# Values of four retention heads and of the spatial gating as one block product with seven products

## The chip, the cores and the metric

The kernel runs on one core of one Trainium2 chip. The metric is the device time of a run in microseconds (us). TensorE (PE in the profile) multiplies matrices, VectorE (DVE), ScalarE (ACT) and GpSimd (POOL) work on rows of 128 partitions, and SyncE (SP) issues transfers. "Layer 0" and "layer 1" are the two layers of the network.

## The reference

Two layers over 512 tokens of 1024 features. What matters here is the input projection of a layer: `proj = rms_norm(h) @ w_in`, cut into nine pieces.

```python
sizes = (D_LRU, D_LRU, D_RET, D_RET, D_RET, D_RET, D_SGU, D_SGU, D_SGU)   # 768, 768, 4 x 768, 3 x 512
x_lru, g_lru, q, k, v, g_ret, u_sgu, v_sgu, g_sgu = jnp.split(proj, split_points, axis=-1)
lru_out = rg_lru(causal_depthwise_conv(x_lru, ...), ...)       # 8 blocks of 96 features
ret_out = retention(q, k, v, positions, ret_norm[i])           # 6 heads of 128, chunks of 128 tokens
sgu_out = spatial_gating(u_sgu, v_sgu, ...)                    # LayerNorm of v_sgu, token mixing in chunks
mixed = concatenate([lru_out * silu(g_lru), ret_out * silu(g_ret), sgu_out * silu(g_sgu)])
h = h + mixed @ w_out[i]
z = rms_norm(h, ple_norm[i])
h = h + sigmoid(z @ w_ple_gate[i]) * (p[i] @ w_ple_proj[i])
```

The values `v` of heads 0 to 3 (512 features) and `v_sgu` (512 features) are two products of the same normed activations (512 tokens by 1024) with two blocks of `w_in` (1024 by 512 each).

## The kernel before, in words

All large products are made in split precision. An operand x becomes a high part (a cast to fp32r) and a low part (x minus the high part), and `mm3` (L172 to L174) adds three products: high by high, high by low, low by high. So every tile of weights costs an ACT cast (L131, `whi`) and a DVE subtraction (L132, `wlo`) before PE may use it. Weights arrive as 82 chunks per layer, most of them 128 x 1024 floats, in the fixed order of `plan()`; `take` hands out the next one, and `prefetch` converts chunks up to four ahead of the one in use. The tags `whi` and `wlo` have four buffers, `raw` (as loaded) has two.

The work of PE is cut into steps (`step`): convert weights ahead, the matmuls, some items of a queue `bg` of background work (`n_bg`, three as a rule), then the eviction of the PSUM accumulator by DVE or ACT. Four accumulators (tag `mm`) go round. The program that builds the kernel orders the instructions of each engine itself, by the source order and by what it takes to be ready, so an instruction can stand far ahead of its place in the source; the order is fixed once built. Each engine runs its own list strictly in order.

A layer goes: six `feat_steps` for `x_lru` with a convolution as eviction (`conv`, L449 to L454, results sent by transfers to the tile `U`, then split into `xc`, L459 and L460); `tok_steps` for `v_sgu` (tokens on the partitions, moving operand 256 weights wide, output `vs`); LayerNorm (`ln_apply`); for each of four column tiles c the steps u(c) and gs(c), with the groups of the recurrence (`lru_group`) of three, three and two blocks ahead of c = 0, 1 and 3; `tok_steps` for the values of heads 0 and 1; `sgu_out` (the gated result `sm` times `w_out`, L622 to L631); six retention heads with k, q and gr steps, and `tok_steps` for values ahead of heads 2 and 4; the output gate; the output projection; the embedding gate. Each `tok_steps` takes two chunks and issues 96 matmuls: 2 halves x 2 token tiles x 8 k tiles x 3.

`norm_stat` and `norm_bcast` give 1/rms as the tile `R` (L288), which every eviction of x_lru needs first. `rope_tables` makes the rotary tables once, as background work that enters the queue after the third x_lru step of layer 0.

Of the kernel before, what the change touches and what calls it, by code (L numbers as in the profile page):

```python
# [26 lines left out]
LRU_AT = {0: 0, 1: 1, 3: 2}  # L27
LRU_GROUPS = [(0, 1, 2), (3, 4, 5), (6, 7)]
# [9 lines left out]
def plan():  # L38
    out = []
    for l in range(DEPTH):  # L40
        out += [(l, "in", OFF["xl"] + P * f, 1024) for f in range(6)]
        for c in range(2):
            out += [(l, "inv", (OFF["vs"] + 256 * c, kh), 1024) for kh in range(2)]
        for c in range(4):
            if c in LRU_AT:
                out += [(l, "lg", LRU_AT[c], 2 * LB * len(LRU_GROUPS[LRU_AT[c]]))]
            out += [(l, "in", OFF["u"] + P * c, 1024), (l, "in", OFF["gs"] + P * c, 1024)]
        for h in range(NH):
            if h % 2 == 0:
                out += [(l, "inv", (OFF["v"] + P * h, kh), 1024) for kh in range(2)]  # L50
            if h == 0:
                out += [(l, "osg", f, 1024) for f in range(4)]
            out += [(l, "in", OFF[n] + P * h, 1024) for n in ("k", "q", "gr")]
# [10 lines left out]

def rows(chunk):
    return LB if chunk[1] == "lg" else P


# the slots of the 40 split operand tiles, by layer
SLOTS = [  # L70
    {"y": range(0, 16), "xc": list(range(16, 28)) + list(range(36, 40)), "lru": range(16, 28), "sgu": range(28, 36), "ret": range(28, 40), "p": range(32, 36)},
    {"y": range(16, 32), "xc": range(0, 16), "lru": range(0, 12), "sgu": range(32, 40), "ret": list(range(32, 40)) + list(range(12, 16)), "p": range(0, 4)},
# [5 lines left out]
def trunk(ctx, tc, a):  # L78
# [7 lines left out]
    def f32(t):  # L86
        return t.bitcast(F32)

    def act_tiles(slots, name):
# [5 lines left out]
    chunks = plan()  # L95
    offs = np.concatenate([[0], np.cumsum([rows(c) * c[3] for c in chunks])])
    st = {"raw": 0, "cv": 0, "use": 0}
    raws, ready = {}, {}
# [4 lines left out]
    def emit_raw():  # L103
        i = st["raw"]
        n, m = chunks[i][3], rows(chunks[i])
        r = wp.tile([P, 1024], F32, tag="raw", name=f"raw{i}", bufs=2)
# [3 lines left out]
        raws[i] = r  # L110
        st["raw"] += 1

    def emit_cv():
        i = st["cv"]
        l, kind, _, n = chunks[i]
        r = raws.pop(i)
# [54 lines left out]
    def mm3(out, wh, wl, xh, xl, first, last):  # L171
        T.matmul(out, wh, xh, start=first, stop=False)  # L172
        T.matmul(out, wh, xl, start=False, stop=False)  # L173
        T.matmul(out, wl, xh, start=False, stop=last)  # L174
# [16 lines left out]
    spt = tp.tile([P, S], F32, tag="r0", name="spt", bufs=3)  # L191
# [8 lines left out]
    posi = tp.tile([P, S], I32, tag="m2", name="posi")  # L200
# [17 lines left out]
    def rsqrt(v, n):  # L218
        """1/sqrt(v) of a small [P, n] tile; a bit seed and three Newton steps."""
# [20 lines left out]
    def norm_square(d, c):  # L240
# [3 lines left out]
        if d == 0:  # L244
            nrm["acc"] = tp.tile([P, S], F32, tag="nacc", name="nacc", bufs=1)
# [9 lines left out]
    def norm_stat(t0=0, nt=4, diag=True):  # L255
# [21 lines left out]
        nrm["dg"] = [tp.tile([P, S], F32R, tag=t, name="n" + t, bufs=b) for t, b in (("dg", 1), ("sq", 2))]  # L277
# [17 lines left out]
    def feat_steps(l, y, kinds, evicts, look=LOOK, n_bg=3, mid=None):  # L295
        """The feature tiles of `kinds` together, one pass over the k tiles."""
# [14 lines left out]
    def tok_steps(l, y, off, evict):  # L311
        """256 features with the tokens on the partitions; evict(half, acc[P, 2, 256])."""
# [22 lines left out]
    def silu_scaled(acc, name):  # L335
        """x * sigmoid(x) of x = acc / rms, in an SBUF tile."""
# [8 lines left out]
    cosT = cp.tile([P, S], F32, name="cosT")  # L345
    sinT = cp.tile([P, S], F32, name="sinT")
# [13 lines left out]
    def rope_tables():  # L360
        ang = tp.tile([P, S], F32, tag="m2", name="ang")
        n1 = tp.tile([P, S], F32, tag="r0", name="n1", bufs=3)
        n2 = tp.tile([P, S], F32, tag="r1", name="n2", bufs=3)
# [56 lines left out]
    # ================= the layers =================  # L420
# [10 lines left out]
    for l in range(DEPTH):  # L431
# [1 line left out]
        U = cp.tile([LB, NB, S], F32, tag="U", name="U")  # L433
        xc = act_tiles(SLOTS[l]["xc"], f"xc{l}_")

        def blocks(c):
            """(block, first row in it, first row of tile c, rows) of the pieces of tile c."""
# [7 lines left out]
        def conv(c):  # L445
            def f(acc):
                u = tp.tile([P, S], F32, tag="r1", name=f"xcv{c}", bufs=3)
# [7 lines left out]
                for b in range(NB):  # L455
                    if P * c < LB * b + LB <= P * c + P:

                        def sp(b=b):
                            SC.copy(xc[b][0][:LB], U[:, b, :])  # L459
                            V.tensor_sub(xc[b][1][:LB], U[:, b, :], f32(xc[b][0])[:LB])  # L460

                        bg.append(sp)

            return f

        feat_steps(l, y, [("in", 0), ("in", P)], [conv(0), conv(1)], mid=norm_finish)
        for c in range(2, 6):
            feat_steps(l, y, [("in", P * c)], [conv(c)])
            if l == 0 and c == 2:
                softplus()  # L470
                bg.extend(rope_tables())
        rn = nrm["rn"]

# [9 lines left out]
        vs = [tp.tile([P, 4, 256], F32, tag="v4", name=f"vs{c}") for c in range(2)]  # L483
# [15 lines left out]
        def ln_apply():
# [7 lines left out]
            for c in range(2):  # L507
                for t in range(4):
                    V.tensor_scalar(vs[c][:, t, :], vs[c][:, t, :], mv[:, t, 0:1], r[:, t : t + 1], op0=ALU.subtract, op1=ALU.mult)
# [9 lines left out]
        def lru_group(g):  # L519
# [3 lines left out]
            def gate_step(gate, b):  # L523
# [10 lines left out]
                def ev():  # L534
                    t = tp.tile([P, S], F32, tag=f"r{gate}", name=f"rg{gate}{b}", bufs=3)[:LB]
# [12 lines left out]
            def tanh_exp():  # L548
                for b in grp:
                    Ts[b] = tp.tile([P, S], F32, tag="r1", name=f"lT{b}", bufs=3)[:LB]  # L550
# [4 lines left out]
            def sqrts():  # L555
                for o, b in enumerate(grp):
                    sTs[b] = tp.tile([P, S], F32, tag="sq" if o < 2 else "dg", name=f"sT{b}", bufs=2 if o < 2 else 1)[:LB]
# [15 lines left out]
        for c in range(2):  # L573
            tok_steps(l, y, OFF["vs"] + 256 * c, vs_evict(c))
# [335 lines left out]
```

## Time and profile before

| what | value |
|---|---|
| three runs | 928.05, 928.16 (median), 928.65 us |
| span of the profiled execution, first to last instruction | 926.7 us |
| PE busy | 912.6 us, 98% of the span |
| DVE busy | 644.3 us, 70% |
| ACT busy | 406.7 us, 44% |
| matmuls | 4786 |

The profile gives the span as the time of the profiled execution; the runs are timed from outside and are some 1.5 us longer than the span. "Busy" for PE counts the time in which some matmul is under way; matmuls overlap, so a group's mean duration is longer than the distance from one start to the next.

### The profile page before, as it was taken

Reading aid. Unit: us, or ns where it says so; the run is one execution under the profiler, and the core shown is the slowest. Engines: PE = TensorE matmul, PEld = TensorE weight load, DVE = VectorE, ACT = ScalarE, POOL = GpSimd, SP = SyncE. Lnnn points to the kernel's source line nnn. Section 1 sums busy time; section 2 is a strip of 40 time slices with the busy share of each in tenths; the row PEclk is TensorE's granted clock in tenths of the full one; section 3 lists DMA queues with packets and bytes.
Section 4 is the critical chain, followed back from the end, with each engine's and each line's share of the span. In section 5 each row is a group of like instructions: output and inputs, shape, how many; then the busy total and the mean of one; then the engine's idle time right before and its main releaser. Section 6 shows DMA issues by size and latency. Waiting matters only on the chain.

```text
span 926.7 us, 12415 instructions
## 1 busy us (share of the span) xinstructions
PE 912.6 (98%) x4786; PEld 778.4 (84%) x4786; DVE 644.3 (70%) x1252; ACT 406.7 (44%) x595; POOL 37.8 (4%) x33
## 2 busy tenths in 40 slices
PE   7999999999999999999999999999999999999997
PEld 5797888888898888888889888988989888888886
DVE  7999996566667774446669699746586777534564
ACT  5349984223233343444434687412323234433353
POOL 3000000000000000110200000000000000011020
PEclk9999999999999999999999999999999999999999
DMA  6452234322222342342334313333222333233312
GB/s 211 128 154 69 61 104 137 93 90 69 92 86 85 109 119 87 108 137 78 104 105 129 104 52 114 98 94 103 71 76 64 111 89 116 86 103 97 125 46 92
DMA packets 31355, 92.60 MB, mean 100 GB/s; under 512 B 4224, under 2 KB 4672, under 8 KB 31296
## 3 DMA queue, kind: packets, MB, share of 16 engines
q1 hardware_dynamic: 27312, 85.42, 29.1%
q10 hardware_dynamic: 3984, 6.38, 2.5%
q8 instruction: 37, 0.61, 0.3%
q14 instruction: 22, 0.18, 0.1%
HBM read 83.40 MB, written 2.10 MB: 92 GB/s over the span
## 4 chain that ended last, share of the span: by engine, by line
PE 88%; DVE 5%; ACT 3%; DMA 1%; issue 1%; DVEq 0%; ACTq 0%
PE acc L174 27%; PE acc L172 27%; PE acc L173 27%; PE sc L680 1%; PE o L705 1%; DVE wlo L132 1%; DMA raw<-in_wall 1%; PE o L707 1%; PE kv L692 1%; PE pp L174 1%; DVE y L237 1%; PE pp L173 1%; PE pp L172 1%; DVE U L567 1%; PE oT L728 1%
## 5 line engine op out<-in xcount | busy, mean ns | idle before, releaser
L131 ACT CAST whi<-raw 128x1024 fp32r<-128x1024 f32 (+1 forms) x160 | 157.9, 990 | 356.7 <-PE acc L173 241.0
L132 DVE TENSOR_TENSOR wlo<-raw,whi 128x1024 fp32r<-128x1024 f32 (+3 forms) x164 | 187.2, 1142 | 104.4 <-ACT whi L131 104.2
L172 PE MATMUL acc<-y,whi 128*128 128x512 f32 x608 | 241.5, 397 | 0.7 <-DVE whi L129 0.6
L173 PE MATMUL acc<-y,whi 128*128 128x512 f32 x608 | 237.7, 391 | 3.0 <-DVE y L237 2.9
L174 PE MATMUL acc<-y,wlo 128*128 128x512 f32 x608 | 237.8, 391 | 0.4 <-DVE wlo L132 0.2
L173 PEld LDWEIGHTS acc<-y,whi 128*128 128x128 f32 x608 | 114.4, 188 | 27.5 <-DVE y L237 5.1
L174 PEld LDWEIGHTS acc<-y,wlo 128*128 128x128 f32 x608 | 114.2, 188 | 25.7 <-DVE wlo L132 1.7
L172 PEld LDWEIGHTS acc<-y,whi 128*128 128x128 f32 x608 | 114.3, 188 | 24.6 <-ACT sq L243 0.7
L172 PE MATMUL acc<-whi,y 128*128 128x256 f32 x320 | 91.3, 285 | 0.0
L174 PE MATMUL acc<-whi,y 128*128 128x256 f32 x320 | 90.6, 283 | 0.0
L173 PE MATMUL acc<-wlo,y 128*128 128x256 f32 x320 | 90.6, 283 | 0.0
L173 PEld LDWEIGHTS acc<-wlo,y 128*128 128x128 f32 x320 | 61.4, 192 | 0.2
L172 PEld LDWEIGHTS acc<-whi,y 128*128 128x128 f32 x320 | 61.4, 192 | 0.2
L174 PEld LDWEIGHTS acc<-whi,y 128*128 128x128 f32 x320 | 61.4, 192 | 0.0
L253 POOL TENSOR_TENSOR nacc<-nacc,sq 128x512 f32<-128x512 f32 (+1 forms) x26 | 36.1, 1388 | 564.7 <-ACT sq L243 564.4
L172 PE MATMUL acc<-z,whi 128*128 128x512 f32 (+1 forms) x144 | 53.0, 368 | 0.0
L174 PE MATMUL acc<-z,wlo 128*128 128x512 f32 (+1 forms) x144 | 52.8, 367 | 0.0
L173 PE MATMUL acc<-z,whi 128*128 128x512 f32 (+1 forms) x144 | 52.7, 366 | 0.0
L173 PE MATMUL acc<-ml,whi 128*128 128x512 f32 x96 | 37.4, 389 | 0.0
L172 PE MATMUL acc<-ml,whi 128*128 128x512 f32 x96 | 37.4, 389 | 0.0
L173 PE MATMUL acc<-rm,whi 128*128 128x512 f32 x96 | 37.4, 389 | 0.0
L174 PE MATMUL acc<-rm,wlo 128*128 128x512 f32 x96 | 37.4, 389 | 0.0
(212 smaller groups left out, 1439.4 us busy)
## 6 DMA issues: line engine op xcount, KB each, us to landing
raw<-in_wall SPq DMA_DIRECT2D x124, 512.0 KB, 3.5
raw<-in_wall SPq DMA_DIRECT2D x32, 384.0 KB, 3.0
hT<-in_xT SPq DMA_DIRECT2D x8, 256.0 KB, 6.1
out_dram<-o SPq DMA_DIRECT2D x8, 256.0 KB, 2.1
U<-xcv ACTq DMA_DIRECT2D x8, 192.0 KB, 2.7
hc<-U ACTq DMA_DIRECT2D x8, 192.0 KB, 2.5
raw<-in_wall SPq DMA_DIRECT2D x4, 256.0 KB, 4.9
U<-xcv ACTq DMA_DIRECT2D x8, 128.0 KB, 2.4
```

The lines of the kernel that those rows point to most:

```text
L131: SC.copy(hi[:m, c], r[:m, c])
L132: V.tensor_sub(lo[:m, c], r[:m, c], f32(hi[:m, c]))
L172: T.matmul(out, wh, xh, start=first, stop=False)
L173: T.matmul(out, wh, xl, start=False, stop=False)
L174: T.matmul(out, wl, xh, start=False, stop=last)
L237: V.scalar_tensor_tensor(x[d][1], h, col(wbase, d), f32(x[d][0]), op0=ALU.mult, op1=ALU.subtract)
L253: (V if d == KD - 1 else G).tensor_add(nrm["acc"][:, c], nrm["acc"][:, c], sq[:, :n])
L567: V.tensor_tensor_scan(u, A, u, 0.0, op0=ALU.mult, op1=ALU.add)
L680: T.matmul(b[:, n, :], k[:, c], q[:, c], start=True, stop=True)
L692: T.matmul(kv[:, n, :], hd["kn"][:, n, :], v4[:, n, e], start=True, stop=True)
L705: T.matmul(o[:, c], hd["s"][:, n, :], v4[:, n, e], start=True, stop=n == 0)
L707: T.matmul(o[:, c], hd["q"][:, c], hd["st"][:, n - 1, :], start=False, stop=True)
```

## The change

`v` of heads 0 to 3 and `v_sgu` are computed as one product of a 2 x 2 block matrix of activations and a 2 x 2 block matrix of weights, by seven block products in place of eight. The activations are cut by tokens (halves of 256) and by alternate k tiles; the weights by the same k tiles and by `v` and `v_sgu`. The seven steps (`fast_step`) come after the x_lru steps, each with two chunks of weights 128 x 1024 and 24 matmuls with a 512-wide moving operand. Four of the seven weight operands (Ta, Tb, Tc, Td) are sums: DVE adds them in place into the loaded tiles (`quad`), and then each chunk is cast and subtracted as others are. Four activation operands (u1, v2, v3, u4) are sums and differences of the scaled h (`fast_sums`), split into high and low tiles `uy`. The blocks are recombined in PSUM and, for three steps, by DVE in SBUF.

Around it: the recurrence runs in four groups of two blocks, ahead of c = 1, ahead of c = 3, inside `sgu_out` and after it; the split of `U` (`lru_split`) moves to just before its group; `sgu_out` follows gs(3) directly; the rotary tables move behind the seven steps of layer 0; `raw` has four buffers and the W11 tiles two of their own (`rawq`); the tags r0 and r1 have two buffers for three; `m1` and the norm's sum share the two buffers of `m2`.

```diff
-LRU_GROUPS = [(0, 1, 2), (3, 4, 5), (6, 7)]
+LRU_GROUPS = [(0, 1), (2, 3), (4, 5), (6, 7)]
+FAST = (("W11", "x11", "X"), ("Ta", "u1", "Y"), ("Tc", "v2", "X"), ("Tb", "v3", "X"), ("Td", "x22", "X"), ("W22", "u4", "Y"), ("W21", "x12", "Z"))
...
+        out += [(l, "fast", (name, c), 1024) for name, _, _ in FAST for c in range(2)]
...
+    def quad(name, c):
+        w11, w12, w22, w21 = [quads.get((q, c)) for q in ("W11", "W12", "W22", "W21")]
+        if name == "Ta":
+            V.tensor_add(w11, w11, w12)
+        elif name == "Tc":
+            V.tensor_add(w11, w11, w22)
+        elif name == "Tb":
+            V.tensor_add(w12, w12, w22)
+        elif name == "Td":
+            V.tensor_add(w11, w11, w21)
...
-            while st["raw"] < min(st["cv"] + 2, len(chunks)):
+            while st["raw"] < min(need[st["cv"]] + 1, len(data)):
...
+        def lru_split(g):
+            def f():
+                for b, x in zip(LRU_GROUPS[g], act_tiles(SLOTS[l]["xc"], f"xc{l}{g}_")):
+                    SC.copy(x[0][:LB], U[:, b, :])
+                    V.tensor_sub(x[1][:LB], U[:, b, :], f32(x[0])[:LB])
...
+        def fast_sums(j):
+            z = [tp.tile([P, S], F32, tag="sq", name=f"fz{j}{i}") for i in range(2)]
+            e = [tp.tile([P, 2, 256], F32, tag="m2", name=f"fe{j}{i}") for i in range(2)]
+            def sums():
+                for i in range(2):
+                    SC.activation(z[i], hT[:, 2 * j + i, :], AF.Copy, scale=col(V_MIX + 8 * l, 2 * j + i))
+                n1, n2 = slice(0, 256), slice(256, 512)
+                V.tensor_sub(e[0][:, 0, :], z[0][:, n2], z[1][:, n2])
+                V.tensor_sub(e[0][:, 1, :], e[0][:, 0, :], z[0][:, n1])
+                V.tensor_sub(e[1][:, 0, :], z[0][:, n1], z[0][:, n2])
+                V.tensor_add(e[1][:, 1, :], z[1][:, n1], e[0][:, 1, :])
+            def split():
+                for i in range(2):
+                    split_to(uy[2 * j + i], e[i].rearrange("p a b -> p (a b)"))
...
         feat_steps(l, y, [("in", 0), ("in", P)], [conv(0), conv(1)], mid=norm_finish)
+        bg.extend([f for j in range(4) for f in fast_sums(j)])
...
+            def pe():                                   # fast_step(i)
+                ws = [take(l, "fast", (name, c)) for c in range(2)]
+                if first:
+                    banks[at] = [bank() for _ in range(2)]
+                for t in range(2):
+                    for k in range(4):
+                        wh, wl = ws[k // 2]
+                        c = slice(512 * (k % 2), 512 * (k % 2) + 512)
+                        xh, xl = fast_operand(xn, k, t)
+                        mm3(banks[at][t], xh, xl, wh[:, c], wl[:, c], first and k == 0, k == 3, more=not first)
+            def ev():
+                for t in range(2):
+                    acc = banks[at][t]
+                    if i == 0:   SC.copy(v4[t], acc)
+                    elif i == 2: SC.copy(vs[t], acc)
+                    elif i == 3:
+                        SC.copy(vs[2 + t], acc)
+                        V.tensor_sub(vs[2 + t], banks["Y"][t], vs[2 + t])
+                        ln_stats(2 + t)
+                    elif i == 4: SC.copy(v4[2 + t], acc)
+                    elif i == 5:
+                        V.tensor_sub(vs[t], acc, vs[t])
+                        ln_stats(t)
+                    elif i == 6: V.tensor_add(v4[t], acc, v4[t])
+            step(pe, ev, n_bg=2)
...
+        drain()
+        for i in range(6):
+            fast_step(i)
+        bg.extend([ln_apply, bias_rows])
+        fast_step(6)
+        drain()
+        if l == 0:
+            bg.extend(rope_tables())
...
-            if c in LRU_AT:
+            if c % 2 == 1:
                 drain()
-                lru_group(LRU_AT[c])
+                lru_group(c // 2)
...
+        drain()
+        sgu_out()            # lru_split(2), lru_group(2), lru_split(3) inside
+        drain()
+        lru_group(3)
         for h in range(NH):
-            if h % 2 == 0:
+            if h == 4:
                 tok_steps(...)
```

`fast_operand` only picks slices of the tiles `y` and `uy`.

More of the change, by code (lines that the diff above doesn't have):

```diff
@@ L62, in plan, with loads @@
     return out
+def loads():
+    out, need = [], []
+    for chunk in plan():
+        l, kind, idx, n = chunk
+        if kind != "fast":
+            out.append(chunk)
+        elif idx[0] == "W11":
+            out.append((l, "quad", ("W11", idx[1]), n))
+        elif idx[0] == "Ta":
+            out.append((l, "quad", ("W12", idx[1]), n))
+        elif idx[0] == "Tc":
+            out.append((l, "quad", ("W22", idx[1]), n))
+        elif idx[0] == "Td":
+            out.append((l, "quad", ("W21", idx[1]), n))
+        need.append(len(out))
+    return out, need
 def rows(chunk):
@@ L87, in f32, with slot_tiles @@
         return t.bitcast(F32)
+    def slot_tiles(slots, name):
+        return [cp.tile([P, S], F32, tag=f"a{s}", name=f"{name}{i}") for i, s in enumerate(slots)]
     def act_tiles(slots, name):
@@ L95, in trunk @@
     chunks = plan()
-    offs = np.concatenate([[0], np.cumsum([rows(c) * c[3] for c in chunks])])
+    data, need = loads()
+    offs = np.concatenate([[0], np.cumsum([rows(c) * c[3] for c in data])])
     st = {"raw": 0, "cv": 0, "use": 0}
-    raws, ready = {}, {}
+    raws, ready, quads = {}, {}, {}
     def halves(i, n):
@@ L104, in emit_raw @@
         i = st["raw"]
-        n, m = chunks[i][3], rows(chunks[i])
-        r = wp.tile([P, 1024], F32, tag="raw", name=f"raw{i}", bufs=2)
+        l, kind, idx, n = data[i]
+        m = rows(data[i])
+        if kind == "quad" and idx[0] == "W11":
+            r = wp.tile([P, 1024], F32, tag="rawq", name=f"rawq{i}", bufs=2)
+        else:
+            r = wp.tile([P, 1024], F32, tag="raw", name=f"raw{i}")
         src = a["wall"][int(offs[i]) : int(offs[i + 1])].rearrange("(p c) -> p c", p=m)
@@ L169, in drain, with mm3 @@
             bg.popleft()()
[L171 to L174, printed above, removed]
+    def mm3(out, wh, wl, xh, xl, first, last, more=False):
+        T.matmul(out, wh, xh, start=first, stop=False, skip_group_check=more)
+        T.matmul(out, wh, xl, start=False, stop=False, skip_group_check=more)
+        T.matmul(out, wl, xh, start=False, stop=last, skip_group_check=more)
     def bank(tag="mm", bufs=4, shape=(P, S), name="acc"):
@@ L244, in norm_square @@
         if d == 0:
-            nrm["acc"] = tp.tile([P, S], F32, tag="nacc", name="nacc", bufs=1)
+            nrm["acc"] = tp.tile([P, S], F32, tag="m2", name="nacc")
             nrm["sq0"] = sq
@@ L446, in f @@
             def f(acc):
-                u = tp.tile([P, S], F32, tag="r1", name=f"xcv{c}", bufs=3)
+                u = tp.tile([P, S], F32, tag="r1", name=f"xcv{c}")
                 xs = tp.tile([P, S], F32, tag="sg", name=f"xs{c}", bufs=3)
@@ L555, in sqrts @@
             def sqrts():
[L556 to L557 removed]
+                for b in grp:
+                    sTs[b] = tp.tile([P, S], F32, tag="sq", name=f"sT{b}")[:LB]
                     SC.activation(sTs[b], Ts[b], AF.Sqrt, bias=cst[:LB, 1:2])
```

155 lines of the change are left out of this document (87 added, 68 removed).

## The prediction

> **What bounds the kernel now.** I read the page's parts 1, 2 and 4 first.
>
> ```profile
> PE 912.6 (98%) x4786; PEld 778.4 (84%) x4786; DVE 644.3 (70%) x1252; ACT 406.7 (44%) x595; POOL 37.8 (4%) x33
> ...
> PE   7999999999999999999999999999999999999997
> ...
> DVE  7999996566667774446669699746586777534564
> ...
> PEclk9999999999999999999999999999999999999999
> ...
> PE 88%; DVE 5%; ACT 3%; DMA 1%; issue 1%; DVEq 0%; ACTq 0%
> ```
>
> PE is the bound of the whole: 98% busy, and the chain of work that ended last is 88% PE. But the DVE line is not even. It stands at 9 in the first slices after the start (layer 0's x_lru, spatial gating and recurrence) and again in the 22nd, 24th and 25th slice (the same stages of layer 1). The change takes work from PE and gives DVE more in exactly these stages, so the second view is the busy time by stage (columns: stretch; its length; busy us and count of PE, PEld, DVE, ACT, POOL; clock; DMA).
>
> ```profile
> 48.80:72.00 23.20, 23.20 (x193) 23.06 (x193) 23.20 (x40) 10.79 (x17) 0.00 (x0) 1.00 0.47 140
> ...
> 146.00:170.00 24.00, 24.00 (x106) 19.85 (x107) 12.59 (x14) 5.91 (x7) 0.00 (x0) 1.00 0.40 131
> ...
> 470.00:483.00 13.00, 12.84 (x61) 10.46 (x60) 6.37 (x30) 3.05 (x3) 0.00 (x0) 1.00 0.27 96
> 483.00:499.30 16.30, 16.30 (x75) 13.52 (x75) 15.66 (x24) 8.60 (x13) 0.00 (x0) 1.00 0.41 119
> 499.30:507.20 7.90, 7.90 (x68) 7.90 (x67) 7.90 (x13) 3.61 (x6) 0.00 (x0) 1.00 0.42 93
> 507.20:522.40 15.20, 15.20 (x127) 14.96 (x126) 6.86 (x16) 5.19 (x8) 0.00 (x0) 1.00 0.29 98
> ```
>
> Two things are read here. First the price of a matmul, as distance between starts: the 256-wide ones of `tok_steps` fill 48.8 to 72.0 with 193, 0.1202 us each; the 512-wide ones of `sgu_out` fill 146 to 170 with 106, 0.2264 us each. Second, DVE's slack: in layer 1 it is full from 483 to 507 and then has 15.20 - 6.86 = 8.3 us free, under the `tok_steps` of v_sgu, which need little of it. PE never waits there, because PE runs ahead while DVE catches up.
>
> The prices, from the groups with shapes kept apart (busy us, mean ns; idle before):
>
> ```profile
> L132 DVE TENSOR_TENSOR wlo<-raw,whi 128x1024 fp32r<-128x1024 f32 x122 | 148.7, 1219 | 74.9 <-ACT whi L131 74.6
> ...
> L460 DVE TENSOR_TENSOR xc<-U,xc 96x512 fp32r<-96x512 f32 x16 | 10.8, 680 | 0.6 <-ACT xc L459 0.6
> ...
> L811 DVE TENSOR_TENSOR pg<-pg,pp 128x256 f32<-128x256 f32 x4 | 1.7, 422 | 1.5 <-ACT pg L810 1.5
> ...
> 103.36 1.88 DVE L540 TENSOR_TENSOR U<-U,rg 96x512 f32<-96x512 f32 x3
> ```
>
> The last row, from the timeline, shows three 512-wide subtractions or products back to back in 1.88 us: each holds DVE for 0.60 us, 0.08 less than its duration. I take the same 0.08 off the others: 1.14 us for 1024 wide, 0.34 for 256 wide.
>
> **The change, part by part.**
>
> *Matmuls.* Per layer four `tok_steps` go (two for v_sgu, two for heads 0 to 3): 4 x 96 = 384 at 0.1202 = 46.2 us. Seven steps of 24 come: 168 at 0.2264 = 38.0 us. PE gains 8.1 us a layer, 16.2 in all. This part is on the path wherever PE is the bound.
>
> *DVE work added, per layer.* Weights: 14 chunks are converted in place of 8, 6 x 1.14 = 6.8 us, and the sums Ta to Td take 4 x 2 x 1.14 = 9.1 us. Activations: 16 sums at 0.34 = 5.4 us and 8 splits at 0.60 = 4.8 us, 10.2 together. Recombination: 6 at 0.60 = 3.6 us. About 30 us a layer, 60 in all; DVE's free 282 us would hold it, but it all falls between the x_lru steps and the end of the seven.
>
> *The start of the second of the seven steps, layer 1.* The first step needs only y and W11. The second, Ta times u1, needs all four rounds of `fast_sums`, both chunks of Ta added and converted, and accumulators that the last two x_lru evictions free. DVE's list up to there begins when R lands:
>
> ```profile
> 483.26 0.59 ACT L288 COPY R<-nR 128x512 f32<-128x512 f32 x1 [0.46 <-PE nR L286]
> ...
> 498.93 0.28 PE L172 MATMUL acc<-whi,y 128*128 128x256 f32 x1
> ...
> 506.45 0.72 DVE L452 SCALAR_TENSOR_TENSOR xcv<-xs,vec,xcv 128x509 f32<-128x509 f32 x1
> ```
>
> PE ends x_lru at 498.93, DVE ends its convolutions at 507.2, full all the way. From this list go six splits of U (L460), 3.6 us, and one LayerNorm instruction, 0.3; to it come 10.2 us of sums and splits and two additions for Ta, 2.3; the last two convolution instructions (1.3) may trail. So Ta's second chunk is ready at 507.2 - 3.9 + 10.2 + 2.3 - 1.3 = 514.5. PE, unhindered, does the first step by 498.93 + 24 x 0.2264 = 504.4 and wants the second chunk six matmuls later, at 505.7. PE waits 8.8 us. Could the sums run earlier, in the 6.6 us that DVE has free between 470 and 483? Their scaled copies of h take the two buffers `sq`, of which the norm's second diagonal (nsq) has one until its product has run, just ahead of R. Bounds: 2.2 us, if those 6.6 are used after all; 12, if ACT, which gets 8 scalings, 8 casts and 2 conversions more in this stretch, holds DVE up as well.
>
> *The same place in layer 0.*
>
> ```profile
> 28.38 0.68 DVE L372 SCALAR_TENSOR_TENSOR angt<-n,angt 128x512 f32<-128x512 f32 x1
> ...
> 30.78 1.23 DVE L132 TENSOR_TENSOR wlo<-raw,whi 128x1024 fp32r<-128x1024 f32 x1 [1.35 <-ACT whi L131]
> ...
> 34.22 0.47 PE L285 MATMUL nR<-ndg,onesr 128*128 128x512 f32 x1 [1.46 <-DVE ndg L280]
> ...
> 48.63 0.28 PE L172 MATMUL acc<-whi,y 128*128 128x256 f32 x1
> ...
> 53.57 0.41 DVE L380 TENSOR_SCALAR n<-angt 128x512 f32<-128x512 f32 x1
> ...
> 60.48 0.73 DVE L452 SCALAR_TENSOR_TENSOR xcv<-xs,vec,xcv 128x509 f32<-128x509 f32 x1
> ```
>
> Here the rotary tables leave. Four of their long instructions stood among the norm's small ones (the row at 28.38 is the last), and DVE then sat 1.35 us idle for weights that came late with two `raw` buffers; without both, R is some 3 us earlier and the PE wait of 1.46 us at nR goes. (These rows also bear out that buffers are given in source order: the next rotary instruction, at 53.57, needed a buffer of tag r1, then free but due to the convolutions first, and did not run in that idle 1.35 us. So `fast_sums` will not overtake nsq either.) List: 61.2, less 3.0, less 1.9 (four rotary instructions after 53) and four splits of U (2.4), plus 10.2 + 2.3 - 1.3 as above, gives 65.1. PE: 48.63 - 1.46 + 5.4 + 1.4 = 54.0. Wait 11.1 us, less the 1.46 that went: 9.6 net. Bounds 3 and 14.
>
> *The later steps of the seven.* DVE needs 4 x 1.14 = 4.6 us for a step with two sums, PE 5.4: covered, if nothing else is in front. One exception: W21 loads into the buffers of W12, which are free only after Tb's conversion, two conversions before W21 is added.
>
> ```profile
> raw<-in_wall SPq DMA_DIRECT2D x124, 512.0 KB, 3.5
> ```
>
> 3.5 us to landing against 2 x 1.14 of DVE work and a cast in between: about 0.8 us a layer, 1.6 in all (0 to 3). The additions queued behind it on DVE wait with it.
>
> *`sgu_out` loses its cover.* Its last operand, sm[3], comes out of gs(3) by a chain of DVE and ACT. Before, `tok_steps` of heads 0 and 1 stood in between:
>
> ```profile
> 131.42 0.28 PE L172 MATMUL acc<-whi,y 128*128 128x256 f32 x1
> ...
> 145.24 0.69 DVE L333 TENSOR_TENSOR sm<-m,sm 128x512 fp32r<-128x512 f32 x1 [0.69 <-ACT sm L332]
> ...
> 145.99 0.50 PE L173 MATMUL acc<-sm,whi 128*128 128x512 f32 x1 [0.22 <-DVE sm L333]
> ...
> 581.23 0.28 PE L172 MATMUL acc<-whi,y 128*128 128x256 f32 x1
> ...
> 591.42 0.69 DVE L333 TENSOR_TENSOR sm<-m,sm 128x512 fp32r<-128x512 f32 x1 [0.69 <-ACT sm L332]
> ...
> 592.75 0.40 PE L172 MATMUL acc<-sm,whi 128*128 128x512 f32 x1
> ```
>
> From the end of gs(3) (the first 256-wide row) to the end of sm[3]: 14.5 us in layer 0, where PE already waited 0.22, and 10.9 in layer 1. What remains as cover are products with sm[0] to sm[2]: nine matmuls, 2.0 us, in source order; 36, 8.2 us, if the built order takes those of all four accumulators first. Four of eight recurrence blocks now come after this point, which lightens DVE in layer 0 about as much as the tables load it, so I take layer 1's 10.9 for both, less 8.2: 2.7 a layer, 5.4 in all. Bounds 0 and 8.9 a layer.
>
> *At nothing:* the regrouped recurrence has the same instructions, and the half that moves behind sgu(3) lies beside matmuls of `sgu_out` and of the first heads, where DVE has slack (12.59 busy of 24.00 us from 146 to 170). Copies of vs and v4 are as many on ACT as before. Loads are as many; their queue gains buffers. Later stages are unchanged.
>
> *Sum:* -16.2 + 8.8 + 9.6 + 1.6 + 5.4 = +9.2 us. The span 926.7 lies 1.5 under the median of the runs, 928.16; what lies around it does not change, so 928.2 + 9.2 = 937.
>
> **The clock.**
>
> ```profile
> L210 PE MATMUL warm<-ones 128*128 128x128 f32 x22 | 5.1, 429 | 1.2 <-DVE ones L203 1.2
> ...
> L832 PE MATMUL acc<-ident,hT 128*128 128x128 f32 x32 | 3.9, 275 | 0.0
> ```
>
> At the start 22 matmuls took 5.1 us of PE, 0.23 each; 32 of the same shape at the end took 3.9, 0.12 each. After that start no PE wait is longer than 2 us and the clock row stays at 9. If a wait of 8 to 11 us brings the slow start back, each costs 22 x 0.11 = 2.4 us, and the time is 942. [...] No run here shows such a wait yet.
>
> **The rivals.**
>
> *DVE is not late* (ends on the faster side). If `fast_sums` and Ta are done when PE reaches the second step, PE alone counts: 928.2 - 16.2 - 1.5 + 1.6 = 912, and with a little wait at `sgu_out` 914. For it: DVE has 6.6 us free before 483 and rotary work did run far ahead of its source place at 28.38. Against it: the buffers above, and a DVE full from 483 to 507 even without the new work. It decides if Ta's second chunk is ready within 2 us of 505.7 in layer 1 and 54.0 in layer 0. Chance 0.27.
>
> *Half late.* Half the wait is covered by overtaking: 928.2 - 16.2 + 9.2 + 1.6 + 2 = 925. Chance 0.15.
>
> *`sgu_out` waits in full.* No reordering: 2 x 8.9 in place of 5.4, so 949. Chance 0.06.
>
> *The clock falls in the waits:* 942. Chance 0.10.
>
> *My forecast,* 937, with its own range 930 to 944: chance 0.42.
>
> **How the numbers follow.** 0.2% is 1.9 us, about what a measurement of this kernel can tell from no change. Faster: all of the first rival and half of the second, 0.34. Within 0.2%: 0.06, from the upper end of the second. Slower: the rest, 0.60. The range runs from 914, the first rival with its small wait, to 948; it leaves out about 0.1 below and 0.06 above.
>
> **What would show it.** In the changed profile: the stage of the seven steps holds 168 matmuls and lasts 38 us of PE work plus the waits; the longest waits of PE are for `wlo` or for an accumulator at the second step, 7 to 12 us in each layer, with DVE full before them; another stands ahead of the first products with sm[3]. Wrong would be: no PE wait above 2 us there; sums that run before R lands; or matmuls with a summed tile at another distance than 0.226 us.

## The result and the profile after

The changed kernel takes 939.57 us (median of four runs, 938.48 to 939.71) against 928.40 for the kernel before on the same chip (928.05 to 929.16): a ratio of 1.0116, 95% interval [1.0102, 1.0131]. It is 1.2% slower. The profiled execution spans 938.0 us, before 926.7: 11.3 us more.

The page of the changed kernel, parts 1, 2 and 4:

```profile
PE 905.9 (97%) x4354; PEld 751.7 (80%) x4354; DVE 705.9 (75%) x1334; ACT 446.9 (48%) x648; POOL 38.9 (4%) x33
...
PE   8979989999999999999998899999999999999996
...
DVE  7999999897858784456769988889786767544564
...
PEclk9989999999999999999999899999999999999998
...
PE 79%; DVE 14%; ACT 3%; issue 2%; POOL 1%; DMA 1%; SPq 0%; ACTq 0%; DVEq 0%
```

PE has 432 matmuls fewer and is still only 6.7 us less busy, partly because some of its products stand 0.43 us apart in place of 0.23 (below). What was 98% of the span is 97%, and the chain of work that ended last has 14% of DVE in it where it had 5%. PE's line has gaps (7 and 8) in the slices where DVE stands at 9, and the clock row drops to 8 in the third and the 23rd slice, one per layer (and in the last slice, at the very end). The waits of PE, and two of the stages (columns of the second view as in the prediction), say where:

```profile
PE acc L220 <- ACT whi L178: 9.0, 2, 4.7
PE acc L221 <- DVE wlo L179: 5.7, 6, 1.4
PE acc L220 <- DVE sxs L388: 2.6, 1, 2.6
...
PE acc L220 <- ACT sm L382: 1.4, 2, 0.8
```
```profile
46.68:96.66 49.98, 42.35 (x172) 32.67 (x170) 49.05 (x83) 26.01 (x35) 0.00 (x0) 0.93 0.37 115
505.80:555.47 49.67, 42.60 (x171) 33.44 (x170) 47.90 (x75) 25.66 (x34) 0.00 (x0) 0.93 0.30 92
...
512.00:516.00 4.00, 0.27 (x1) 0.00 (x0) 4.00 (x8) 1.95 (x4) 0.00 (x0) 1.00 0.22 66
```

The two long rows are the seven steps of layer 0 and layer 1, 170 products each (168, and two for the row that the LayerNorm's bias needs, 0.9 us, which stood right behind the `tok_steps` of v_sgu before, at 71.67 and 521.97; the rows count one or two more that began earlier). 168 at the spacing forecast, 0.2264, are 38.0 us; the stages last 50.0 and 49.7. DVE is busy 49.05 of 49.98. The four `tok_steps` that went took 46.2, so each stage is longer than what it replaces, by 3.8 and 3.5 us (2.9 and 2.6 without the bias row). The last row is the middle of the wait in layer 1: PE stands still, and DVE has no gap.

The wait itself, PE and then DVE, from the timeline of layer 1 (start, duration, engine, line, output <- inputs, idle before and what ended it):

```profile
511.25 1.02 PE L623 MATMUL rs<-ws,ones 128*128 128x512 f32 x2
516.56 0.56 PE L220 MATMUL acc<-whi,uy 128*128 128x512 f32 x1 [4.28 <-ACT whi L178]
518.48 0.79 PE L221 MATMUL acc<-wlo,uy 128*128 128x512 f32 x1 [1.36 <-DVE wlo L179]
519.07 0.63 PE L222 MATMUL acc<-whi,uy 128*128 128x512 f32 x1
519.50 0.63 PE L220 MATMUL acc<-whi,uy 128*128 128x512 f32 x1
...
523.73 0.85 PE L220 MATMUL acc<-whi,uy 128*128 128x512 f32 x3
```
```profile
492.65 0.41 DVE L503 TENSOR_TENSOR fe<-fz,fz 128x256 f32<-128x256 f32 x1
...
513.21 0.41 DVE L506 TENSOR_TENSOR fe<-fz,fe 128x256 f32<-128x256 f32 x1
...
514.21 1.21 DVE L151 TENSOR_TENSOR rawq<-rawq,raw 128x1024 f32<-128x1024 f32 x1
...
520.74 1.21 DVE L153 TENSOR_TENSOR rawq<-rawq,raw 128x1024 f32<-128x1024 f32 x1
521.87 0.74 DVE L540 SCALAR_TENSOR_TENSOR xcv<-xs,vec,xcv 128x510 f32<-128x510 f32 x1
522.53 1.22 DVE L179 TENSOR_TENSOR wlo<-rawq,whi 128x1024 fp32r<-128x1024 f32 x1
```

The first activation sum starts at 492.65, the last ends at 513.6, Ta's first addition at 514.21, its second chunk is converted at 522.53 + 1.22 = 523.75. The releaser that the profile names, ACT's `whi`, is only the last link: ACT casts a tile that DVE has just added. Up to then PE had the products of the first chunk, and did them 0.43 us apart in place of 0.23. By count, its first product with the second chunk's high part is at 522.91 and the first with its low part (L221) at 524.42, with no idle time between them.

From the starts of each step, counted in the timeline, the loss against 24 x 0.2264 is 8.7 us in the second step of both layers (5.9 and 5.6 us of it PE stands still, most of the rest is the slow products); 1.3 (layer 0) and 0.9 (layer 1) in the third; and 1.0 and 1.15 in the fifth, Td with x22. With the bias row's 0.9 that makes the 12.0 and 11.6 by which the stages exceed 38.0.

### The profile page after: what moved, and what is told of

The parts are those of the page before. It is cut to its first block, busy times and chain, and to the rows that moved or that the text cites. A ratio compares the mean times of both kernels' runs of the same rounds, so it can differ in the third digit from the quotient of the medians.

```text
span 938.0 us, 11683 instructions
## 1 busy us (share of the span) xinstructions
PE 905.9 (97%) x4354; PEld 751.7 (80%) x4354; DVE 705.9 (75%) x1334; ACT 446.9 (48%) x648; POOL 38.9 (4%) x33
## 4 chain that ended last, share of the span: by engine, by line
PE 79%; DVE 14%; ACT 3%; issue 2%; POOL 1%; DMA 1%; SPq 0%; ACTq 0%; DVEq 0%
PE acc L221 24%; PE acc L222 23%; PE acc L220 23%; DVE wlo L179 3%; DVE xcv L540 2%; PE sc L807 1%; PE o L830 1%; DVE uy L383 1%; PE o L832 1%; PE kv L818 1%; ACT rg L646 1%; PE pp L222 1%; PE pp L221 1%; PE pp L220 1%; POOL nacc L303 1%
## 5 line engine op out<-in xcount | busy, mean ns | idle before, releaser
L178 ACT CAST whi<-raw 128x1024 fp32r<-128x1024 f32 (+2 forms) x158 | 153.8, 979 | 289.6 <-PE acc L221 211.9
L220 PE MATMUL acc<-y,whi 128*128 128x512 f32 x608 | 242.2, 398 | 4.2 <-DVE sxs L388 2.6
L221 PE MATMUL acc<-y,whi 128*128 128x512 f32 x608 | 238.0, 392 | 2.3 <-DVE y L287 2.2
L179 DVE TENSOR_TENSOR wlo<-raw,whi 128x1024 fp32r<-128x1024 f32 (+3 forms) x162 | 181.3, 1121 | 77.1 <-ACT whi L178 76.6
L220 PEld LDWEIGHTS acc<-y,whi 128*128 128x128 f32 x608 | 114.7, 189 | 28.6 <-DVE sxs L388 3.0
L221 PEld LDWEIGHTS acc<-y,whi 128*128 128x128 f32 x608 | 114.7, 189 | 27.0 <-DVE y L287 4.3
L220 PE MATMUL acc<-z,whi 128*128 128x512 f32 (+1 forms) x144 | 53.0, 368 | 0.0
L221 PE MATMUL acc<-z,whi 128*128 128x512 f32 (+1 forms) x144 | 52.7, 366 | 0.0
L221 PE MATMUL acc<-wlo,y 128*128 128x256 f32 (+1 forms) x112 | 37.0, 330 | 1.6 <-DVE wlo L179 1.6
L220 PE MATMUL acc<-rm,whi 128*128 128x512 f32 x96 | 37.3, 389 | 0.0
L221 PE MATMUL acc<-rm,whi 128*128 128x512 f32 x96 | 37.3, 389 | 0.0
L220 PE MATMUL acc<-ml,whi 128*128 128x512 f32 x96 | 37.3, 389 | 0.0
L221 PE MATMUL acc<-ml,whi 128*128 128x512 f32 x96 | 37.3, 389 | 0.0
L222 PE MATMUL acc<-ml,wlo 128*128 128x512 f32 x96 | 37.3, 389 | 0.0
L222 PE MATMUL acc<-whi,y 128*128 128x256 f32 (+1 forms) x112 | 36.8, 329 | 0.0
L220 PE MATMUL acc<-whi,y 128*128 128x256 f32 (+1 forms) x112 | 36.8, 331 | 0.0
L220 PE MATMUL acc<-whi,uy 128*128 128x512 f32 x64 | 26.2, 423 | 9.0 <-ACT whi L178 9.0
```

The source lines that it names most:

```text
L178: SC.copy(hi[:m, c], r[:m, c])
L179: V.tensor_sub(lo[:m, c], r[:m, c], f32(hi[:m, c]))
L220: T.matmul(out, wh, xh, start=first, stop=False, skip_group_check=more)
L221: T.matmul(out, wh, xl, start=False, stop=False, skip_group_check=more)
L222: T.matmul(out, wl, xh, start=False, stop=last, skip_group_check=more)
```

## The experiments

The theory: DVE's list, in strict order from R to the conversion of Ta's second chunk, is the path; a microsecond of summing in it costs about a microsecond. Rivals: the waits come from the order of the seven products (PE has nothing else to do at that place); the half-speed clock after the wait (granted clock 0.50) is what costs; or the surroundings (regrouped recurrence, moved tables) cost, not the products. Ratios are against the kernel before, run on the same chip.

**The weight sums left out.** In `quad`:

```diff
-        if name == "Ta":
-            V.tensor_add(w11, w11, w12)
...
-        elif name == "Td":
-            V.tensor_add(w11, w11, w21)
```

> The eight additions a layer that make Ta, Tb, Tc and Td are left out (the weights go into the steps unsummed, so the values are not the reference's); casts, subtractions, matmuls and all else stay. Theory 1 (DVE's list in front of the second of the seven steps is too long): Ta's two additions, 2.3 us, leave that list, and the small waits of 0.7 to 1.1 us at later sums go as well, about 2 us; so some 4 us a layer less, 939.6 - 8 = 932. Theory 2 (the wait is for the cast on ACT and the four weight buffers, whatever DVE does): at most 2 us in all, 938.

928.52 us, ratio 0.9998 [0.9989, 1.0007]. The 11 us are gone with 8 additions a layer, 9.1 us of DVE each layer; I had expected 8. One wait in each layer's seven steps is left:

```profile
PE acc L213 <- DVE wlo L171: 6.1, 2, 3.5
```

**The activation sums left out.** In `fast_sums` (the scaled h is split as it is):

```diff
-                V.tensor_sub(e[0][:, 0, :], z[0][:, n2], z[1][:, n2])
-                V.tensor_sub(e[0][:, 1, :], e[0][:, 0, :], z[0][:, n1])
-                V.tensor_sub(e[1][:, 0, :], z[0][:, n1], z[0][:, n2])
-                V.tensor_add(e[1][:, 1, :], z[1][:, n1], e[0][:, 1, :])
...
-                    split_to(uy[2 * j + i], e[i].rearrange("p a b -> p (a b)"))
+                    split_to(uy[2 * j + i], z[i])
```

> Left out: the 16 sums and differences of the scaled h per layer (the scaled h itself is split into uy instead; so u1, v2, v3, u4 are wrong operands). All casts, splits, scalings and the weight sums stay. Theory DVE: the wait at the second of the seven steps is the length of DVE's list ahead of it; 16 x 0.34 = 5.4 us a layer leave it, so that the wait there (4.7 + 1.1 us in layer 0, 4.3 + 1.4 in layer 1) all but goes, and the time is 929 to 930 in place of 939.6. Rival ACT: those waits end on whi, which ACT writes; if the scalings and casts of ACT, with two buffers for the scaled h, set the pace, the wait stays within 2 us and the time is 936 or more.

929.77 us, ratio 1.0009 [1.0000, 1.0019]: 9.8 us less, for 10.8 us of DVE work removed. ACT's own work is unchanged here, so its length does not set the pace. The waits did not all but go as I had written: 2.73 us remain in layer 0 at the second step and 2.45 + 1.11 in layer 1, now at the second chunk's `wlo`.

**Both left out.**

> Left out: the sums of activations and the sums of weights, both. The seven steps, their casts and splits and the recombination stay. Theory DVE: no wait of more than 1 us is left inside the seven steps; they last 38 to 39 us a layer; without weight sums alone the time was 928.5 with waits of 3.5 and 2.7 us left, so 928.5 - 6.2 = 922. Rival: the seven steps are bound by something besides the sums (conversions of 14 chunks in place of 8, the recombination), and the time stays above 926.

919.06 us, ratio 0.9891 [0.9876, 0.9906]. The two single gains, 11.0 and 9.8, add up to 20.8; together they give 20.5. A microsecond of sums was worth 0.6 (weights) to 0.9 us (activations). Layer 0's stage, with one wait above 0.4 us in it (0.51 for `wlo`):

```profile
47.17:86.91 39.74, 39.23 (x171) 31.84 (x170) 35.79 (x64) 23.41 (x31) 0.00 (x0) 1.00 0.47 144
```
39.74 is 38.0, the bias row and some 0.8. So the conversions of 14 chunks in place of 8, the splits and the recombination are covered; the sums are what is not. The time came out 3 us below what I expected, for I had subtracted only the two waits, 6.1 us, that were left without the weight sums. Without the weight sums the second step loses more than its wait (3.5 and 2.7 us), 5.8 and 4.8 us by the starts of the steps, because the clock falls after it. In layer 1 without weight sums, after the wait of 2.67 us that ends at 510.00:

```profile
510.00:511.00 1.00, 0.99 (x4) 0.84 (x5) 1.00 (x2) 1.00 (x2) 0.00 (x0) 1.00 0.00 0
...
512.00:513.00 1.00, 1.00 (x3) 0.50 (x2) 1.00 (x2) 0.00 (x0) 0.00 (x0) 0.50 0.00 0
```

There the second chunk is ready when PE resumes, so that the slow products lie on the path: the loss is 2.3 and 2.1 us more than the waits, some 1.6 of it from eight products 0.43 us apart.

**Another order of the products.** W21 times x12, which needs no sum of either kind, second in place of last; W21 is loaded twice.

```diff
-FAST = (("W11", "x11", "X"), ("Ta", "u1", "Y"), ("Tc", "v2", "X"), ("Tb", "v3", "X"), ("Td", "x22", "X"), ("W22", "u4", "Y"), ("W21", "x12", "Z"))
+FAST = (("W11", "x11", "X"), ("W21", "x12", "Z"), ("Ta", "u1", "Y"), ("Tc", "v2", "X"), ("Tb", "v3", "X"), ("Td", "x22", "X"), ("W22", "u4", "Y"))
```

> W21 times x12, which needs no sum of weights and none of activations, becomes the second of the seven steps; its chunks are loaded once more for Td (1 MB more a layer). [...] Theory 2: the wait only moves behind the new second step: 938 to 940.

939.17 us, ratio 1.0108 [1.0090, 1.0125]: no gain. The timeline of layer 1:

```profile
514.39 0.50 PE L225 MATMUL acc<-wlo,y 128*128 128x512 f32 x1 [2.66 <-DVE wlo L183]
516.86 0.50 PE L224 MATMUL acc<-whi,y 128*128 128x512 f32 x1 [0.83 <-DVE xs L541]
525.21 0.77 PE L224 MATMUL acc<-whi,uy 128*128 128x512 f32 x1 [4.20 <-DVE v L599]
```

PE had a product with nothing to sum, and waited inside it for its `wlo`, whose conversion stands behind the sums in DVE's list, and then again for an accumulator that DVE empties. A product to fill the hole still needs DVE: in this order the wait only moves. The order also has a price of its own, since it holds all four accumulators ahead of Ta. DVE converted Ta's first chunk at 522.7 and its second at 524.5 and emptied the accumulator at 525.1, so up to 2.5 us of the last wait may be the accumulator's; an order without this price was not tried.

**Keeping the clock up.** Four idle fp32 products (eight matmuls in the trace, 3.70 us in layer 0) between the first and the second step:

```diff
+                if i == 1:
+                    junk = bank("st", 1, name="junk")
+                    for _ in range(4):
+                        T.matmul(junk, ones, v4[0], start=True, stop=True)
```

> Four idle products (ones times the first v tile, 512 wide, about 0.9 us each, result unused) are put on PE between the first and the second of the seven steps, where PE waits. Theory 3 (part of the loss is the clock that falls in the wait): the granted clock stays at 1.00 and the ten matmuls at 0.43 us take 0.23: 2 us a layer less, 935.6, while DVE's part of the wait stays. If the clock costs nothing, 939.6; if the idle products themselves come late, up to 1 us a layer more.

939.99 us, ratio 1.0118 [1.0100, 1.0137] (the traced execution took 942.04). The clock held (1.00 in the windows 52 to 60 and 512 to 524), and no time was won: the products ran faster and PE waited longer. Waits in the changed kernel were 5.7 us in all for `wlo` and 9.0 for `whi`; here:

```profile
PE acc L221 <- DVE wlo L179: 8.2, 6, 2.0
PE acc L220 <- ACT whi L178: 3.8, 4, 1.1
```

The waits for `whi` are shorter because the idle products, some 3.5 us a layer, fill them. Those for `wlo` are longer, the one for W21 above all: 1.3 and 2.0 us in place of 0.7 and 0.9. So at the second step the half-speed products cost PE time that it would have waited anyway.

**The activation sums on GpSimd.** `V.` becomes `G.` in the four lines of `sums`.

> The 16 sums of activations a layer run on GpSimd in place of DVE; all else as changed. Theory 1 (what counts is the length of DVE's own list up to the end of the seven steps): 5.4 us a layer leave it, and the run loses 5.4 to 6.4 a layer of its waits: 939.6 - 11 = 928.5. Against it (theory 5: the sums are late anyway on GpSimd, at 0.74 us for 256 wide by its 512-wide additions of 1.44, in rounds that wait for ACT and DVE, or hold DVE up at the shared memory): 935 or more.

944.74 us, ratio 1.0167 [1.0148, 1.0185]: worse by 5 us. The wait at the second step grew to 6.8 and 6.5 us. GpSimd in layer 1:

```profile
499.66 1.27 POOL L503 TENSOR_TENSOR fe<-fz,fz 128x256 f32<-128x256 f32 x1 [3.14 <-ACT fz L501]
...
504.39 1.77 POOL L506 TENSOR_TENSOR fe<-fz,fe 128x256 f32<-128x256 f32 x1
```
```profile
509.36 1.23 DVE L540 SCALAR_TENSOR_TENSOR xcv<-xs,vec,xcv 128x510 f32<-128x510 f32 x1
512.57 0.69 DVE L383 TENSOR_TENSOR uy<-fe,uy 128x512 fp32r<-128x512 f32 x1 [1.98 <-ACT uy L382]
```

Two things cost. A sum that takes DVE 0.42 takes GpSimd 0.72 at best and up to 1.77 beside a busy DVE, and DVE's convolution (0.74) took 1.23 beside it. And each round of sums hands over from ACT to GpSimd to ACT to DVE through two buffers, so DVE, which was full, now waits 1.98 us for its split. With the second chunk's weight additions on GpSimd too:

> As the run before, and the second chunk's addition of Ta, Tb, Tc and Td on GpSimd too (some 2.9 us each by its 512-wide additions of 1.44), the first chunk's on DVE. Theory 1: another 4 x 1.14 = 4.6 us a layer off DVE's list; the waits of the seven steps are almost gone, 920 to 924. Theory 5: GpSimd has 12 + 11.5 us a layer in a chain, its additions come late: no better than the run before.

952.75 us, ratio 1.0260 [1.0234, 1.0286]; the wait at the second step is 10.7 and 9.8 us.

**Eight plain products.** The same 512-wide steps with the eight plain block products, no sums and no recombination; all the rest of the change (regrouped recurrence, moved tables, buffers) stays.

> The same kernel as changed, but with the eight plain block products in place of seven: 512-wide moving operands, no sums of weights or activations, four accumulators, four steps of 48 matmuls; recurrence in groups of two, moved tables and sgu_out directly behind gs(3) stay. PE: 192 x 0.2264 = 43.5 us a layer against 46.2 before. Theory 1: the loss lies in the sums, so 928.4 - 5.4 and what the surroundings cost. Theory 4 (the surroundings cost by themselves the 4 us a run that the stages outside the seven steps lost): 927. If they cost nothing: 923. If the surroundings, not the sums, were the cause of the whole loss: 935 or more.

929.14 us, ratio 1.0003 [0.9994, 1.0013]. No wait is left in the product stage: with 24 products a layer more (10.9 us in all) the kernel is 10.4 us faster than the changed one. But its time is only that of before, though 192 products at 0.2264 (43.5 us) stand where four `tok_steps` took 46.2. Part of the difference is lost in layer 0's gating, as in the changed kernel:

```profile
PE acc L203 <- DVE sxs L371: 2.6, 1, 2.6
```

**Eight products, tables back.** The rotary tables enter the queue after the third x_lru step, as before the change:

```diff
                 softplus()
+                bg.extend(rope_tables())
...
-        if l == 0:
-            bg.extend(rope_tables())
```

> The eight plain products, with the rotary tables back at their old place in layer 0 (background work after the third x_lru step). Theory 4 (of the surroundings it is the tables that cost: the first u eviction needs a buffer of tag m2, which the tables' angle holds till they end, and PE waits for the accumulators behind it): the 2.6 us wait and the smaller ones in layer 0's gating go, some 4 to 5 us, the start of layer 0 loses the 1.9 us it had gained: 929.1 - 2 to 3 = 926.5. If it is the regrouped recurrence or m1 and m2 in the same two buffers: 931, since the start loses and the waits stay.

925.42 us, ratio 0.9960 [0.9947, 0.9973]: faster than both kernels. Layer 0's gating stage, first with the tables behind the products, then with them back:

```profile
100.00:126.00 26.00, 23.43 (x100) 18.54 (x99) 24.93 (x42) 18.94 (x24) 0.00 (x0) 0.93 0.28 87
```
```profile
100.00:126.00 26.00, 26.00 (x123) 21.34 (x122) 20.23 (x29) 18.15 (x25) 0.00 (x0) 1.00 0.28 82
```

DVE goes from 24.93 busy us of 26 to 20.23, and PE from 23.43 to all 26.

**Eight products, tables first** (emitted ahead of the first x_lru step):

> The eight plain products, with the rotary tables put ahead of the first x_lru step in the source, beside the norm of layer 0. Theory 4: the waits in layer 0's gating go as in the run before, and the x_lru evictions are not mixed with table work; the start loses up to 2 us where the tables stand among the norm's small instructions: 925 to 927. If the tables at the start hold the norm up for their whole 13 us: 935.

934.10 us, ratio 1.0054 [1.0036, 1.0072]: ahead of everything the tables delay the norm, the last case of the expectation.

```profile
40.73 0.77 PE L318 MATMUL nR<-nsgm,onesr 128*128 128x512 f32 x1 [4.03 <-DVE nsgm L313]
```

**The changed kernel, tables back.** The same edit on the seven products:

> The changed kernel whole, with the rotary tables back in the queue after the third x_lru step of layer 0. Theory DVE: what layer 0 wins behind the seven steps (4 to 5 us of waits) it gives back ahead of them: four rotary instructions of 0.48 us or more behind the x_lru steps and the later R make the wait at the second step 3 to 5 us longer, and 1.5 us of wait for nR come back; 938 to 941. Rival: the two terms are independent, as with eight products (3.7 us won): 936.

944.19 us, ratio 1.0159 [1.0144, 1.0174]: 4.6 us slower than with the tables moved, more than I gave it.

```profile
47.04:107.04 60.00, 47.97 (x172) 35.35 (x171) 57.81 (x93) 29.09 (x39) 0.00 (x0) 0.86 0.29 90
```

This row is layer 0's stage: 60.0 us in place of 50.0. Fourteen long table instructions (L419, 9.6 us) now stand among the sums and conversions of the seven steps, where the changed kernel has none; the waits for `whi` and `wlo` in the whole run sum to 19.0 us in place of 14.7, and the mean clock of the stage is 0.86 in place of 0.93. So the tables' place is worth +3.7 us with eight products and -4.6 with seven. Without sums:

> As the kernel without sums of activations and weights, and the rotary tables back in the queue after the third x_lru step of layer 0. Theory: the moved tables cost 3.7 us by themselves (they did with eight products), so 922 - 4 = 918, and what the matmuls save is then to be seen: before less 16.2, plus about 6 of smaller waits. The prediction's rival in which DVE is not late said 912 to 914. Rival: the tables at their old place bring back the wait for nR and make DVE late ahead of the second step in layer 0, and nothing is won: 921 or more.

919.86 us, ratio 0.9901 [0.9885, 0.9918], the same as with the tables moved (919.06). The waits in layer 0's gating go (2.6 us for `sxs` and 0.6 for `rg`), and 1.83 and 2.31 us at the second step take their place. The prediction's rival of 912 to 914 is not reached by either place.

The three pairs of runs agree on what the tables' place does. By the starts in the traces, in us (tables behind the products, then back):

| kernel | stage of layer 0 begins | stage lasts | from its end to layer 1's R |
|---|---|---|---|
| seven products | 46.68, 47.04 | 49.98, 60.00 | 393.46, 387.81 |
| eight products | 46.94, 50.61 | 44.42, 43.52 | 393.38, 387.77 |
| seven, no sums | 47.17, 46.93 | 39.74, 45.29 | 393.41, 387.94 |

Behind the products the tables cost the rest of layer 0 some 5.6 us, whatever the products; ahead of them they cost the start or the stage, and most where the sums already fill DVE.

## Why the prediction was right, and where its terms were off

The forecast was 937.0 and slower; measured 939.6. Its likeliest case was the one that happened, but the sum is nearer than its terms: `sgu_out` was 4.0 us too large and the second step of layer 0 2.4 us, and the tables, set at nothing, cost some 5.6. That these nearly cancel is luck. By its steps, in us of the span. The measured parts: layer 0's x_lru ends at 46.68 in place of 48.63 (-1.95); the stages +3.8 and +3.5; layer 1's R comes 6.86 later (490.12 against 483.26), so that the rest of layer 0 took 6.86 + 1.95 - 3.8 = +5.0; and +0.95, what is left of the 11.3, the rest of layer 1:

| step of the prediction | forecast | measured |
|---|---|---|
| matmuls, each layer | -8.1 | spacing 0.2267 (24 in 5.44 us); holds |
| second step, layer 1 | +8.8 | 8.7, and 0.9 at the third |
| second step, layer 0 | +11.1, less 1.46 at nR | 8.7, and 1.3 at the third; start -1.95 |
| W21's load, each layer | +0.8 | 1.0 and 1.15 in the step before it, where its additions stand |
| stage as a whole against what went | +3.8 and +1.5 | +3.8 and +3.5 |
| rest of layer 0 (`sgu_out` +2.7, tables and recurrence 0) | +2.7 | +5.0 |
| rest of layer 1 (`sgu_out` +2.7) | +2.7 | +0.95 |

The measured stages hold the bias row's 0.9 us, which has left the rests. That the stage of layer 0 comes out at the forecast +3.8 is chance too: 2.4 us less in the second step, against 1.3 in the third and the bias row.

*The second step.* The reading was DVE's list after R. It said that Ta's second chunk is ready at 514.5, 30.7 us after R's end (483.26 + 0.59). R's copy in the changed kernel:

```profile
490.12 0.59 ACT L338 COPY R<-nR 128x512 f32<-128x512 f32 x1 [0.50 <-PE nR L336]
```

From 490.71 to 523.75 are 33.0 us, 2.4 more. Two items stand ahead that I had let trail: Tc's addition at 520.74 (1.21) and the convolution at 521.87. And I took six splits of U off the list up to 507.2, where the trace before has five (the sixth begins at 507.10): 0.6 us. In return PE did not want the second chunk "six matmuls later" but twelve, 1.4 us; the built order does the first chunk's products of both token tiles first, and the bias row, 0.9 us, stands ahead of them. The misses nearly cancel. In layer 0 the reading of the list was right, 65.1:

```profile
63.87 1.22 DVE L179 TENSOR_TENSOR wlo<-rawq,whi 128x1024 fp32r<-128x1024 f32 x1
```

There I had 2.4 us too much, mainly because the twelve products and the bias row bring PE to the chunk 2.2 us later. The sign that I named, waits of 7 to 12 us, shows as 5.9 and 5.6 us of standstill; the rest of the 8.7 is mostly slow products. That `fast_sums` will not overtake the norm is borne out: the first sum starts at 492.65, after R.

*W21.* The wait for the transfer is there, at the addition for Td:

```profile
534.50 1.23 DVE L157 TENSOR_TENSOR rawq<-rawq,raw 128x1024 f32<-128x1024 f32 x1 [0.51 <-DMA raw<-in_wall]
```
```profile
539.24 0.50 PE L221 MATMUL acc<-wlo,y 128*128 128x512 f32 x1 [0.86 <-DVE wlo L179]
```

0.51 us on DVE and 0.86 on PE, against 0.8 forecast.

*`sgu_out`.* Over-sized. PE waited 0.8 us in layer 0 and 0.6 in layer 1 for sm[3] (1.4 in two waits, above), not 2.7:

```profile
163.75 0.62 ACT L382 CAST sm<-m 128x512 fp32r<-128x512 f32 x1 [2.66 <-DVE m L717]
...
164.40 0.69 DVE L383 TENSOR_TENSOR sm<-m,sm 128x512 fp32r<-128x512 f32 x1
...
164.42 0.98 PE L220 MATMUL acc<-sm,whi 128*128 128x512 f32 x3 [0.82 <-ACT sm L382]
```

The cover is near the better one that I named: behind gs(3), whose products end at 154.80 and 608.28, stand 36 products with sm[0] to sm[2] in layer 0 (and two of xc, 0.45 us) and 31 in layer 1. What I had too long is the chain. I counted 10.9 us to the end of sm[3]'s low part, which DVE writes (L383). PE's first products with sm[3] (L220) need only its high part, which ACT writes (L382), and that was there 9.6 us behind gs(3) in layer 0 and 7.7 in layer 1.

*"At nothing".* This is the term that failed, in layer 0. I set the tables that move behind the seven steps against the recurrence blocks that leave the same stretch, about as much, and so at nothing; the slack that I named, from 146 to 170, is where those blocks go. But the tables run before, in the gating:

```profile
96.66:127.19 30.53, 27.96 (x131) 22.53 (x130) 28.80 (x56) 16.96 (x21) 0.00 (x0) 1.00 0.30 99
```
```profile
126.46 0.68 DVE L388 TENSOR_TENSOR sxs<-acc,R 128x512 f32<-128x512 f32 x1
127.06 0.68 DVE L419 SCALAR_TENSOR_TENSOR ang<-n,ang 128x512 f32<-128x512 f32 x1
...
127.19 0.50 PE L220 MATMUL acc<-y,whi 128*128 128x512 f32 x1 [2.57 <-DVE sxs L388]
```

DVE is busy 28.80 of 30.53 us there, the eviction `sxs` comes late between table rows (L419), and PE stops 2.57 us for its accumulator. After that wait the clock falls for 3.4 us (127.73 to 131.15, below), some 1.6 us more. That moving the tables back takes these waits away was shown in all three pairs above, 5.6 us of the rest of layer 0. The regrouped recurrence was not tried by itself; with the tables back, 0.6 us at `sgu_out` and 0.3 at `xc` remain in each layer, so it costs little.

*The clock.* The rival of 942 said that the wait brings the slow clock back. It does:

```profile
56.05:62.88 6.83, 3.87 (x8) 2.77 (x9) 6.83 (x9) 2.90 (x3) 0.00 (x0) 0.50 0.18 38
...
127.73:131.15 3.42, 3.42 (x9) 2.65 (x8) 2.68 (x5) 3.39 (x6) 0.00 (x0) 0.50 0.14 43
...
518.48:523.34 4.86, 4.86 (x12) 3.79 (x13) 4.86 (x6) 2.91 (x3) 0.00 (x0) 0.50 0.25 54
```

At the waits of 4.74 and 4.28 us the granted clock is 0.50 for 6.83 us (56.05 to 62.88 and 516.85 to 523.68), PE is busy in 3.9 and 5.5 us of them, and in layer 1 twelve products take 4.86 us where 2.7 would do. The price I gave it, about 2.4 us a wait, was right there for PE's own time. It did not reach the end time, because DVE needed those microseconds for the second chunk in any case; keeping the clock up won nothing. (Without the weight sums, where DVE is ready sooner, some 2 us a layer did.) The second row is a fall that I had not looked for, behind the wait of 2.57 us in layer 0's gating; whether its 1.6 us reached the end time was not tested by itself. The prediction looked for the slow clock behind waits of 8 to 11 us; waits of 2.57 us here and of 2.67 us without the weight sums had it behind them too.

*DVE not late* (912 to 914) was the wrong rival for the whole kernel: its condition, Ta ready when PE arrives, is nearly met only in the kernel without sums (one wait of 0.51 us in layer 0's stage), which reached 919. What it misses is about the 5.6 us of the tables.

## What to carry to other kernels

Seven products for eight saved 10 us on the path (929.1 against 919.1 without the sums) and cost 20.5 us (919.1 against 939.6) for some 29 us of sums that stood in a full DVE list: before trading matmuls for sums, count the other engine's list from the last thing that it must wait for to the first operand that PE needs, not its mean load. While that engine was full here, neither the other order of PE's work that was tried, nor a warm clock at the wait, nor GpSimd for part of the sums helped; less work in the list did. Work moved out of the list has a price where it goes: the tables cost 5.6 us behind the products. The part worth keeping was eight plain products with the wider moving operand and the tables at their old place, 925.4 us, 0.40% [0.27%, 0.53%] under the kernel before; the operand's share of these 3.2 us was not measured apart from the buffers and the regrouped recurrence that stay in it.

## What the runs showed of the hardware

- In the changed kernel the granted clock was 0.50 in three stretches before its end, each in or behind a PE wait: 56.05 to 62.88 (wait of 4.74 us), 127.73 to 131.15 (2.57) and 516.85 to 523.68 (4.28), with 512-wide products 0.43 us apart in place of 0.227. With four idle fp32 products in the wait at the second step it stayed at 1.00 there (52 to 60 and 512 to 524).
- The stretches last 3.42 or 6.83 us and begin 71.68 and 389.12 us apart. The length of a wait alone did not decide. With the idle products, the wait of 2.57 us in the gating brought no fall and one of 2.00 us at 539.95 did. Without the weight sums one of 2.67 us did, 1.5 us after PE had resumed; without the activation sums one of 2.45 us did not (the clock is 1.00 from 510 to 514). In the 3.42 us ahead of a fall PE was busy for 0.52, 0.85 and 0.29 us in the changed kernel and for 1.50 in layer 1 without the weight sums (the row below). What decides is not shown.

```profile
508.09:511.51 3.42, 1.50 (x6) 1.24 (x7) 3.42 (x6) 3.32 (x5) 0.00 (x0) 1.00 0.07 21
```

- GpSimd and DVE slowed each other. With the sums on GpSimd, 256-wide sums took 0.72 to 1.77 us there (0.74 at 494.96 and 511.14, where DVE stood idle; 1.77 at 504.39, where it worked), and the convolution's DVE instructions a mean of 0.83 to 0.86 against 0.74 to 0.75 without it. With weight additions on GpSimd too, four of these DVE instructions took 2.85 to 2.88 us; each ended 0.55 us after an addition of GpSimd that had begun before it (one pair below; what held DVE is not shown):

```profile
513.77 2.73 POOL L155 TENSOR_TENSOR raw<-raw,raw 128x1024 f32<-128x1024 f32 x1
```
```profile
514.17 2.88 DVE L540 SCALAR_TENSOR_TENSOR xcv<-xs,vec,xcv 128x511 f32<-128x511 f32 x1
```

With the sums on GpSimd the run took 944.7 us against 939.6.
